# Query and key heads of the sparse attention: transposed two at a time in float32, split into parts from PSUM

## The chip, the cores and the metric

One core of a Trainium2 chip runs one decoder layer. The metric is the device time of one execution in microseconds (us).

## The reference, cut to what matters

The layer is h + half a SwiGLU, then a mixer of two head groups, then half a SwiGLU and a gated embedding; width 1024, 512 tokens, float32 throughout. The change is in the first head group, native sparse attention (NSA): 8 query heads of 64 in two groups of 4, and 2 key/value heads (one for each group) for each of two kinds, "selected" and "window".

```python
q_a = partial_rope(rmsnorm(split_heads(qa, N_HEADS_NSA), q_norm_nsa[i]), cos, sin)
k_slc = partial_rope(rmsnorm(split_heads(ksl, N_KV_NSA), k_norm_slc[i]), cos, sin)
k_win = partial_rope(rmsnorm(split_heads(kwn, N_KV_NSA), k_norm_win[i]), cos, sin)
...
s_c = jnp.einsum('bkgqd,bknd->bkgqn', qq, k_cmp) * scale
...
s_s = jnp.einsum('bkgqd,bkqnd->bkgqn', qq, kg) * scale
...
s_w = jnp.einsum('bkgqd,bknd->bkgqn', qq, kw) * scale
```

With 512 tokens, all 8 blocks are selected and the window covers all, so both kinds are full causal attention with different keys and values. The second head group (FoX, 8 heads) and the two SwiGLU blocks are not touched.

## The kernel before

Every product is made from float32 numbers split into two parts of type float32r: hi, a rounded copy (made by ScalarE), and lo, the rest (a subtraction on VectorE). A general product takes three matmuls (hi hi, hi lo, lo hi). A head has only 64 dimensions, so in attention its hi part and its lo part lie above each other in the 128 partitions: a query operand A holds hi and lo, and there are two key operands, B with hi and lo and B with the halves exchanged. Two matmuls over 128 partitions then give all four products.

The code does not write instructions in order. Each call goes to a planner (class Plan): `record` keeps the operation, its cost by formula and what it depends on; two instructions of different engines that touch the same PSUM tile are always put in order, whatever they do. `weave` mixes several streams of work, those with less TensorE cost so far first. `issue` then fixes the order on each engine by a greedy schedule with these costs, within a window of 440 operations, and `emit` (line 306) issues the instructions. So nearly every instruction in the profile stands at L306, and groups are told apart by engine, operation and tiles. Engines run their queues in order.

Names of tiles: `acc` and `gub` are the two sorts of PSUM bank, four of each; `k` is a 4 KB tile, here the operands A and B (also others); `hl` holds the two parts of heads before they are transposed, two buffers; `w` is a working tile of 2 KB; `st`, `hi` and `lo` are loaded weights and their parts; `s`, `r`, `cs` are small tiles; `x` is an 8 KB tile.

The mixer goes in this order: a projection for compression; then keys and values (`kv_project`), followed by the queries of group 0 (`q_project(0)`), woven with the compression's own products; then the compressed attention of group 0 and its first head pair, woven with the queries of group 1; then further pairs, woven with FoX projections and FoX pairs. For each of four tiles of 128 tokens a projection ends in `kv_done` or `q_done`: ScalarE scales the sums out of PSUM, squares them, VectorE sums the squares, POOL takes the inverse root (tile `s`, with `mhalf`), VectorE scales by it and by the gain, and POOL rotates the first 16 dimensions (`rope`, tiles `r` and `w`). What stands after the rotation is what changes:

- `split_heads` makes hi (ScalarE) and lo (VectorE) of four heads, side by side for each head, in `hl`;
- TensorE transposes each head's 128 columns (hi and lo together) into PSUM, four transposes into two `gub` banks;
- for queries (`qT`), ScalarE copies each bank into A in one go; for keys, three copies of a bank (one whole, two exchanged halves) go to B, for one kind on ScalarE and for the other on VectorE.

`A[g][a]` holds the heads 2a and 2a+1 of group g, and `B[kind][i]` both key heads of a kind. `cmp_attention` and `nsa_pair` read these.

Of the kernel before, what the change touches and what calls it, by code (L numbers as in the profile page):

```python
# [7 lines left out]
F32 = mybir.dt.float32  # L8
# [6 lines left out]
P = 128  # L15
# [293 lines left out]
class Layer:  # L309
# [471 lines left out]
    def parts(hl, hd, i):  # L781
        return hl[:, hd, i:i + 2].rearrange("p a d -> p (a d)").bitcast(F32)

    def qT(self, hl, heads, dst, t):

        nc = self.nc
        ps = self.gub()
        for i, hd in enumerate(heads):
            nc.tensor.transpose(ps[:, i * P:(i + 1) * P], self.parts(hl, hd, 0), self.ident)
        nc.scalar.copy(dst[:, :, t * P:(t + 1) * P], ps[:, :2 * P].rearrange("p (a c) -> p a c", a=2))  # L790

    def vsplit(self, src, dst, t):

# [182 lines left out]
    def cmp_attention(self, A, t, g, o):  # L976

        nc = self.nc
        ps = self.gub()
        pv = ps[:, :256].rearrange("p (h a n) -> p h a n", h=4, a=2)  # L980
        for hd in range(4):
            a = A[hd // 2][:, hd % 2, t * P:(t + 1) * P]
            nc.tensor.matmul(pv[:, hd], lhsT=a, rhs=self.kcT[:, :, g * 32:g * 32 + 32], start=True, stop=True)
        s = self.misc((P, 4, 32), "cs", 2)
        nc.vector.tensor_tensor(s, pv[:, :, 0], self.cmask[:, t, None, :].to_broadcast([P, 4, 32]), ALU.add)
        nc.vector.tensor_tensor(s, s, pv[:, :, 1], ALU.add)
        m, rs = self.small(4), self.small(4)
        nc.vector.tensor_reduce(m, s, axis=AX.X, op=ALU.max)
        bc = lambda x: x[:, :, None].to_broadcast([P, 4, 32])
        nc.gpsimd.tensor_tensor(s, s, bc(m), ALU.subtract)  # L990
        nc.scalar.activation(s, s, AF.Exp)
        nc.vector.tensor_reduce(rs, s, axis=AX.X, op=ALU.add)
        nc.vector.reciprocal(rs, rs)
        nc.vector.scalar_tensor_tensor(rs, rs, self.cval[:, t:t + 1], self.gates[:, t, 4 * g:4 * g + 4, 0],
                                       op0=ALU.mult, op1=ALU.mult)
        nc.gpsimd.tensor_tensor(s, s, bc(rs), ALU.mult)
        pt = self.gub()
        nc.tensor.transpose(pt[:, :P], s.rearrange("p h n -> p (h n)"), self.ident)
        pr = self.misc((P, 2, P), "cp", 2, F32R)
        nc.scalar.copy(pr[:, 0], pt[:, :P])  # L1000
        nc.vector.tensor_sub(pr[:, 1], pt[:, :P], pr[:, 0].bitcast(F32))
        po = self.gub()
        for i, (x, y) in enumerate(((0, 0), (0, 1), (1, 0))):
            nc.tensor.matmul(po[:, :256], lhsT=pr[:, x], rhs=self.vbd[:, g, y], start=(i == 0), stop=(i == 2))
        nc.scalar.copy(o[:, t, 256 * g:256 * g + 256], po[:, :256])
        yield
# [61 lines left out]
    def mix(self, xT, rs_in, o_nsa, o_fox, nsa_out):  # L1068
        nc = self.nc
        G, V = nc.gpsimd, nc.vector  # L1070
# [21 lines left out]
        B, Vt = {}, {}  # L1092

        def kv_project():
            for kind in range(2):
                Vt[kind] = self.k4((P, 2, NT, P), F32R)
                B[kind] = [self.k4((P, 2, 512), F32R) for _ in range(2)]

            def kv_done(t, ps):
                u = self.w2()  # L1100
                nc.scalar.mul(u, ps, rs_in[t])
                uv = u.rearrange("p (a s h d) -> p a s h d", a=2, s=2, h=2)
                for kind in range(2):
                    self.vsplit(uv[:, kind, 1], Vt[kind], t)
                xn = self.w2()[:, :256]
                x4 = xn.rearrange("p (a h d) -> p a h d", a=2, h=2)
                sq, ss = self.w2()[:, :256], self.small(4)
                nc.scalar.activation(sq.rearrange("p (a h d) -> p a h d", a=2, h=2), uv[:, :, 0], AF.Square)
                V.tensor_reduce(ss, sq.rearrange("p (n d) -> p n d", n=4), axis=AX.X, op=ALU.add)
                r = self.rstd(ss, 64, 4).rearrange("p (a h) -> p a h", a=2)  # L1110
                V.tensor_tensor(x4, uv[:, :, 0], r[:, :, :, None].to_broadcast([P, 2, 2, 64]), ALU.mult)
                V.tensor_tensor(x4, x4, self.gkv[:, :, None, :].to_broadcast([P, 2, 2, 64]), ALU.mult)
                xn = xn.rearrange("p (n d) -> p n d", n=4)
                self.rope(G, xn, t, 4)
                hl = self.split_heads(xn, 4, 2)
                cols = slice(t * P, (t + 1) * P)
                for kind in range(2):
                    tp = self.gub()
                    for i in range(2):
                        nc.tensor.transpose(tp[:, i * P:(i + 1) * P], self.parts(hl, 2 * kind + i, 0), self.ident)  # L1120
                    k = tp[:, :256].rearrange("p (a c) -> p a c", a=2)
                    copy = nc.scalar.copy if (t + kind) % 2 else V.tensor_copy
                    copy(B[kind][0][:, :, cols], k)
                    copy(B[kind][1][0:64, :, cols], k[64:128])
                    copy(B[kind][1][64:128, :, cols], k[0:64])
            yield from self.project(xT, [(768, 512)], kv_done, "v")

        A = {}

        def q_project(g):  # L1130
            A[g] = [self.k4((P, 2, 512), F32R) for _ in range(2)]

            def q_done(t, ps):
                u = self.w2()[:, :256].rearrange("p (h d) -> p h d", h=4)
                nc.scalar.mul(u, ps[:, :256].rearrange("p (h d) -> p h d", h=4), rs_in[t])
                xn = self.w2()[:, :256].rearrange("p (h d) -> p h d", h=4)
                self.head_norm(V, u, xn, self.gq[:, None, :].to_broadcast([P, 4, 64]))
                self.rope(G, xn, t, 4)
                hl = self.split_heads(xn, 4, 2)
                for i in range(2):  # L1140
                    self.qT(hl, (2 * i, 2 * i + 1), A[g][i], t)
            yield from self.project(xT, [(256 * g, 256)], q_done, f"q{g}")

        def cmp_group(g):
# [3 lines left out]
        def nsa_pair(g, a):  # L1148
            for kind in range(2):
                rs = self.rs_tile()  # L1150
                hd = 4 * g + 2 * a
                cols = slice(64 * hd, 64 * hd + 128)

                def write(ps, coef):
                    tmp = self.w2()
                    tv = tmp.rearrange("p (t h d) -> p t h d", t=NT, h=2)
                    V.tensor_mul(tv, ps, coef)
                    G.tensor_tensor(o_nsa[:, :, cols], o_nsa[:, :, cols],
                                    tmp.rearrange("p (t c) -> p t c", t=NT), ALU.add)
                run = lambda par: self.unit([(A[g][a][:, par], B[kind][i][:, g]) for i in range(2)], Vt[kind][:, g],  # L1160
                                            rs, par)
                yield from self.pair([run, run],
                                     rs, self.gates[:, :, hd:hd + 2, 1 + kind], write)
# [30 lines left out]
        def f_pair(p):  # L1194
# [7 lines left out]
            def write(ps, coef):  # L1202
# [9 lines left out]
                    self.forget_rows())  # L1212
        nc.weave(chain(kv, q_project(0)), cmp)
        streams = dict(c0=cmp_group(0), c1=cmp_group(1), n00=nsa_pair(0, 0), n01=nsa_pair(0, 1), n10=nsa_pair(1, 0),
                       n11=nsa_pair(1, 1), q1=q_project(1), out=nsa_out)
        for p in range(4):
            streams[f"F{p}"], streams[f"f{p}"] = f_project(p), f_pair(p)
# [335 lines left out]
```

## Time and profile before

| | us |
|---|---|
| median of 3 runs | 1086.06 (1085.07 to 1086.37) |
| profiled execution | 1086.81 |
| its span, first to last instruction | 1085.0 |

| engine | busy us | share of the span | instructions |
|---|---|---|---|
| PE (TensorE matmul) | 1068.3 | 98% | 6723 |
| PEld (its weight loads) | 963.0 | 89% | 6723 |
| DVE (VectorE) | 767.7 | 71% | 1320 |
| ACT (ScalarE) | 579.4 | 53% | 1115 |
| POOL (GpSimd) | 183.6 | 17% | 314 |

Times in rows count from the start of the span. The granted TensorE clock was 0.999 of full speed. Matmuls overlap each other (the next starts before the last one ends), so a busy time near the length of a stretch can hide small gaps. The mixer lies between about 310 and 690 us; the tiles of keys and queries that the change touches between 389 and 470 us.

### The profile page before, as it was taken

Reading aid. Unit: us, or ns where it says so; the run is one execution under the profiler, and the core shown is the slowest. Engines: PE = TensorE matmul, PEld = TensorE weight load, DVE = VectorE, ACT = ScalarE, POOL = GpSimd, SP = SyncE. Lnnn points to the kernel's source line nnn. Section 1 sums busy time; section 2 is a strip of 40 time slices with the busy share of each in tenths; the row PEclk is TensorE's granted clock in tenths of the full one; section 3 lists DMA queues with packets and bytes.
Section 4 is the critical chain, followed back from the end, with each engine's and each line's share of the span. In section 5 each row is a group of like instructions: output and inputs, shape, how many; then the busy total and the mean of one; then the engine's idle time right before and its main releaser. Section 6 shows DMA issues by size and latency. Waiting matters only on the chain.

```text
span 1085.0 us, 17692 instructions
## 1 busy us (share of the span) xinstructions
PE 1068.3 (98%) x6723; PEld 963.0 (89%) x6723; DVE 767.7 (71%) x1320; ACT 579.4 (53%) x1115; POOL 183.6 (17%) x314
## 2 busy tenths in 40 slices
PE   9999999999999999999999999999999999999998
PEld 6789899988997878999999888889989998899887
DVE  5976378744774777989889786977537784487473
ACT  5544145522543768988888864645315552255351
POOL 1010000000000246554344610310000000000000
PEclk9999999999999999999999999999999999999999
DMA  8496356643444622302102241686535674333421
GB/s 269 138 236 195 97 138 186 186 131 99 116 118 123 216 68 75 85 6 60 41 21 75 74 161 51 221 224 167 174 97 144 187 183 132 102 108 122 152 107 67
DMA packets 76420, 139.79 MB, mean 129 GB/s; under 512 B 13616, under 2 KB 33600, under 8 KB 76080
## 3 DMA queue, kind: packets, MB, share of 16 engines
q1 hardware_dynamic: 71376, 120.76, 34.3%
q0 software_dynamic: 4960, 17.91, 9.4%
q8 instruction: 53, 0.87, 0.3%
q14 instruction: 31, 0.25, 0.1%
HBM read 132.23 MB, written 6.42 MB: 128 GB/s over the span
## 4 chain that ended last, share of the span: by engine, by line
PE 82%; DVE 6%; ACT 3%; DMA 3%; POOL 3%; issue 3%; SPq 0%; ACTq 0%; POOLq 0%; DVEq 0%
PE acc L306 52%; PE gub L306 30%; DVE k L306 2%; DVE lo L306 2%; POOL s L306 1%; ACT k L306 1%; DVE w L306 1%; ACT w L306 1%; DMA pt<-in_quarters 1%; DMA k<-in_x 1%; POOL r L306 1%; DMA gq<-in_q_norm_nsa 1%; POOL w L306 1%; ACT hi L306 1%; DVE pt L306 0%
## 5 line engine op out<-in xcount | busy, mean ns | idle before, releaser
L306 PE MATMUL acc<-hi,k 128*128 128x512 f32 (+1 forms) x832 | 262.8, 389 | 1.7 <-ACT k L306 1.2
L306 ACT CAST hi<-st 128x1024 fp32r<-128x1024 f32 (+4 forms) x150 | 148.6, 991 | 179.6 <-PE acc L306 93.3
L306 DVE TENSOR_TENSOR lo<-st,hi 128x1024 fp32r<-128x1024 f32 (+4 forms) x150 | 171.6, 1146 | 64.7 <-ACT hi L306 64.4
L306 PE MATMUL acc<-hi,x 128*128 128x384 f32 (+3 forms) x720 | 199.4, 349 | 0.3 <-ACT hi L306 0.3
L306 PEld LDWEIGHTS acc<-hi,k 128*128 128x128 f32 x832 | 155.9, 188 | 33.0 <-ACT k L306 2.0
L306 PE MATMUL acc<-lo,k 128*128 128x512 f32 (+1 forms) x432 | 163.9, 383 | 0.5 <-DVE lo L306 0.5
L306 ACT CAST hi<-pt 128x1024 fp32r<-128x1024 f32 x68 | 71.3, 1049 | 159.9 <-PE acc L306 90.3
L306 PE MATMUL gub<-x,hi 128*128 128x256 f32 x816 | 147.4, 282 | 0.1
L306 PE MATMUL acc<-x,hi 128*128 128x256 f32 x816 | 147.2, 282 | 0.0
L306 DVE TENSOR_TENSOR lo<-pt,hi 128x1024 fp32r<-128x1024 f32 x68 | 83.1, 1222 | 80.3 <-ACT hi L306 80.3
L306 PE MATMUL gub<-k,hi 128*128 128x512 f32 (+1 forms) x560 | 138.2, 338 | 1.1 <-ACT hi L306 1.1
L306 PEld LDWEIGHTS acc<-hi,x 128*128 128x128 f32 x720 | 127.1, 189 | 11.1 <-ACT hi L306 0.4
L306 PEld LDWEIGHTS gub<-x,hi 128*128 128x128 f32 x816 | 126.1, 189 | 0.8 <-DVE w L306 0.3
L306 PE MATMUL acc<-lo,x 128*128 128x384 f32 (+3 forms) x360 | 125.1, 348 | 1.7 <-DVE lo L306 1.7
L306 PEld LDWEIGHTS acc<-x,hi 128*128 128x128 f32 x816 | 125.6, 188 | 0.0
L306 PE MATMUL gub<-x,lo 128*128 128x256 f32 x408 | 115.3, 283 | 0.0
L306 PE MATMUL acc<-x,lo 128*128 128x256 f32 x408 | 115.3, 283 | 0.0
L306 POOL DMA_DIRECT2D pt<-in_quarters x34 | 29.8, 877 | 477.4 <-DMA pt<-in_quarters 240.4
L306 PEld LDWEIGHTS gub<-k,hi 128*128 128x128 f32 x560 | 96.3, 189 | 12.6 <-ACT hi L306 1.6
L306 PE MATMUL gub<-k,lo 128*128 128x512 f32 (+1 forms) x280 | 94.5, 338 | 0.4 <-DVE lo L306 0.4
L306 PEld LDWEIGHTS acc<-lo,k 128*128 128x128 f32 (+1 forms) x432 | 79.4, 184 | 15.6 <-DVE lo L306 0.8
L306 PEld LDWEIGHTS gub<-x,lo 128*128 128x128 f32 x408 | 76.9, 188 | 0.0
(163 smaller groups left out, 1714.6 us busy)
## 6 DMA issues: line engine op xcount, KB each, us to landing
st<-in_quarters SPq DMA_DIRECT2D x51, 512.0 KB, 3.5
st<-in_ffn_wd SPq DMA_DIRECT2D x44, 512.0 KB, 4.9
pt<-in_quarters SPq DMA_DIRECT2D x34, 512.0 KB, 4.5
pt<-in_quarters POOLq DMA_DIRECT2D x34, 512.0 KB, 6.5
st<-in_quarters SPq DMA_DIRECT2D x32, 256.0 KB, 4.9
st<-in_w_in SPq DMA_DIRECT2D x48, 128.0 KB, 2.4
st<-in_first SPq DMA_DIRECT2D x16, 256.0 KB, 3.8
st<-in_w_in SPq DMA_DIRECT2D x8, 512.0 KB
```

Source lines behind the costliest of these rows:

```text
L306: getattr(getattr(self.nc, op.eng), m)(*a, **k)
```

## The change

The heads are no longer split before the transpose. `turned` transposes two heads of float32 numbers at once: the 64 columns of two neighbouring heads make 128 columns, so four heads take two transposes into one `gub` bank, and of each pair the even head comes out on partitions 0 to 63 and the odd one on 64 to 127. The parts are made from PSUM: for each half, ScalarE copies hi to the same partitions and VectorE subtracts hi from the PSUM value and writes lo to the other 64. The operands are therefore sorted by the half a head came out on: `A[g][par]` holds the heads par and par + 2 of group g (odd heads with lo above hi), and `B[g][i]` the key head g of both kinds. For keys the second operand is made in the same way from PSUM: hi on the other side by ScalarE, lo by VectorE. The readers in `cmp_attention` and `nsa_pair` index accordingly. FoX keeps `split_heads`.

```diff
-    def qT(self, hl, heads, dst, t):
-
-        nc = self.nc
+    def turned(self, x):
+
         ps = self.gub()
-        for i, hd in enumerate(heads):
-            nc.tensor.transpose(ps[:, i * P:(i + 1) * P], self.parts(hl, hd, 0), self.ident)
-        nc.scalar.copy(dst[:, :, t * P:(t + 1) * P], ps[:, :2 * P].rearrange("p (a c) -> p a c", a=2))
+        for i in range(2):
+            self.nc.tensor.transpose(ps[:, i * P:(i + 1) * P], x[:, 2 * i:2 * i + 2].rearrange("p a d -> p (a d)"),
+                                     self.ident)
+        return ps[:, :2 * P].rearrange("p (a c) -> p a c", a=2)
+
+    def qT(self, x, dst, t):
+
+        pv = self.turned(x)
+        for par in range(2):
+            r, o = slice(64 * par, 64 * par + 64), slice(64 - 64 * par, 128 - 64 * par)
+            d = dst[par][:, :, t * P:(t + 1) * P]
+            self.nc.scalar.copy(d[r], pv[r])
+            self.nc.vector.tensor_sub(d[o], pv[r], d[r].bitcast(F32))
...
         for hd in range(4):
-            a = A[hd // 2][:, hd % 2, t * P:(t + 1) * P]
+            a = A[hd % 2][:, hd // 2, t * P:(t + 1) * P]
...
                 self.rope(G, xn, t, 4)
-                hl = self.split_heads(xn, 4, 2)
+                pv = self.turned(xn)
                 cols = slice(t * P, (t + 1) * P)
-                for kind in range(2):
-                    tp = self.gub()
-                    for i in range(2):
-                        nc.tensor.transpose(tp[:, i * P:(i + 1) * P], self.parts(hl, 2 * kind + i, 0), self.ident)
-                    k = tp[:, :256].rearrange("p (a c) -> p a c", a=2)
-                    copy = nc.scalar.copy if (t + kind) % 2 else V.tensor_copy
-                    copy(B[kind][0][:, :, cols], k)
-                    copy(B[kind][1][0:64, :, cols], k[64:128])
-                    copy(B[kind][1][64:128, :, cols], k[0:64])
+                for g in range(2):
+                    r, o = slice(64 * g, 64 * g + 64), slice(64 - 64 * g, 128 - 64 * g)
+                    k = pv[r]
+                    nc.scalar.copy(B[g][0][r, :, cols], k)
+                    V.tensor_sub(B[g][0][o, :, cols], k, B[g][0][r, :, cols].bitcast(F32))
+                    nc.scalar.copy(B[g][1][o, :, cols], k)
+                    V.tensor_sub(B[g][1][r, :, cols], k, B[g][0][r, :, cols].bitcast(F32))
...
                 self.rope(G, xn, t, 4)
-                hl = self.split_heads(xn, 4, 2)
-                for i in range(2):
-                    self.qT(hl, (2 * i, 2 * i + 1), A[g][i], t)
+                self.qT(xn, A[g], t)
...
-                run = lambda par: self.unit([(A[g][a][:, par], B[kind][i][:, g]) for i in range(2)], Vt[kind][:, g],
+                run = lambda par: self.unit([(A[g][par][:, a], B[g][i][:, kind]) for i in range(2)], Vt[kind][:, g],
                                             rs, par)
```

## Rows read from the trace of the kernel before

**Rows 1.** The page: busy time of engines; shares of the chain that ended last.
```profile
PE 1068.3 (98%) x6723; PEld 963.0 (89%) x6723; DVE 767.7 (71%) x1320; ACT 579.4 (53%) x1115; POOL 183.6 (17%) x314
...
PE 82%; DVE 6%; ACT 3%; DMA 3%; POOL 3%; issue 3%; SPq 0%; ACTq 0%; POOLq 0%; DVEq 0%
```
**Rows 2.** Busy time by stretch: length, then PE, PEld, DVE, ACT, POOL.
```profile
385.00:395.00 10.00, 8.89 (x41) 6.96 (x40) 5.51 (x16) 4.05 (x11) 5.10 (x12) 1.00 0.01 2
425.00:435.00 10.00, 9.34 (x76) 8.68 (x76) 7.97 (x26) 7.80 (x19) 9.23 (x20) 1.00 0.32 78
435.00:445.00 10.00, 9.14 (x72) 8.23 (x70) 9.47 (x44) 9.82 (x38) 5.43 (x15) 1.00 0.21 55
445.00:465.00 20.00, 20.00 (x147) 19.28 (x146) 18.74 (x53) 18.55 (x55) 10.18 (x19) 1.00 0.33 82
...
445.00:645.00 200.00, 197.85 (x1290) 181.75 (x1289) 178.49 (x506) 170.44 (x483) 86.74 (x139) 1.00 0.22 64
```
**Rows 3.** The chain in order of time, 385 to 475 us: start, length, what.
```profile
389.32 0.41 ACT hl L306
389.76 0.44 DVE hl L306
...
390.24 0.66 PE gub L306 x4
...
431.00 0.41 ACT hl L306
...
436.35 0.42 ACT hl L306
436.79 0.42 DVE hl L306
...
442.23 0.39 PE gub L306
```
**Rows 4.** Waits, 360 to 440 us: total, times, longest.
```profile
ACT hl L306 <- POOL w L306: 3.9, 4, 1.5
...
PE gub L306 <- DVE hl L306: 1.5, 2, 1.1
```
**Rows 5.** Timeline of PE, transposes of a query tile: start, length, what.
```profile
427.59 0.66 PE L306 MATMUL gub<-ident,hl 128*128 128x128 f32 x4 [0.38 <-DVE hl L306]
428.08 1.04 PE L306 MATMUL gub<-ident,w 128*32 128x128 f32 x8
428.88 0.36 PE L306 MATMUL acc<-hi,x 128*128 128x256 f32 x1
```
**Rows 6.** Timeline of ACT, a query tile's split and the instruction after it.
```profile
455.63 0.40 ACT L306 CAST hl<-w 128x256 fp32r<-128x256 f32 x1
455.94 0.40 ACT L306 ACTIVATE w<-w,s 128x128 f32<-128x128 f32 x1
```
**Rows 7.** Timeline, reads of PSUM banks: a key tile; later `norm_pairs`.
```profile
390.71 1.29 DVE L306 CAST k<-gub 128x256 fp32r<-128x256 f32 x3 [0.20 <-PE gub L306]
...
390.93 1.13 ACT L306 CAST k<-gub 128x256 fp32r<-128x256 f32 x3 [0.89 <-PE gub L306]
...
671.34 0.62 ACT L306 CAST k<-gub 128x256 fp32r<-128x256 f32 x2
...
671.73 0.75 DVE L306 TENSOR_TENSOR k<-gub,k 128x256 fp32r<-128x256 f32 x2 [1.48 <-ACT k L306]
...
672.80 0.65 ACT L306 CAST k<-gub 128x256 fp32r<-128x256 f32 x2
```
**Rows 8.** Groups by form, whole span: busy us, mean ns, idle before.
```profile
L306 DVE CAST k<-gub 64x256 fp32r<-64x256 f32 x40 | 16.7, 417 | 0.6 <-PE gub L306 0.2
L306 ACT CAST k<-gub 64x256 fp32r<-64x256 f32 x40 | 14.6, 366 | 0.4
L306 DVE TENSOR_TENSOR hl<-w,hl 128x256 fp32r<-128x256 f32 x28 | 12.0, 430 | 7.8 <-ACT hl L306 7.6
L306 DVE TENSOR_TENSOR k<-gub,k 128x256 fp32r<-128x256 f32 x24 | 9.3, 414 | 3.3 <-ACT k L306 3.3
```

## The prediction

> **What bounds the kernel now.** I read the page first, for the engines' shares [rows 1]: TensorE has work in flight for 98% of the span, and the chain that ended last runs 82% over it. Whatever takes TensorE time away where TensorE sets the pace is therefore worth its full price. But 98% is a mean, so the second view was the busy time by stretch around the change [rows 2]. Three stretches differ. From 385 to 395 us and from 425 to 445 us (keys, then the queries of group 0) TensorE is busy only 8.89, 9.34 and 9.14 of 10 us, and at 435 to 445 us ScalarE (9.82) and VectorE (9.47) are fuller than it is. From 445 to 465 us (queries of group 1 beside the first attention pair) TensorE is at 20.00 of 20. From 445 to 645 us, the rest of the mixer, it is at 197.85 of 200. Matmuls overlap, so even 9.1 of 10 hides small gaps. The third view, the chain in order of time for the early stretch, shows what the keys and queries wait for [rows 3]: at 389.32 us a split on ScalarE (0.41), at 389.76 the subtraction on VectorE (0.44), and only then the four transposes. At 431.00 and 436.35 us the split of a query tile is on the chain again, on ScalarE, and once more its subtraction at 436.79. So here the chain is one of small steps on several engines, and TensorE waits; TensorE's own waits name the same steps [rows 4].
>
> **What the change touches.** Twelve token tiles go through it: four of keys (kv_done), four for each of the two query groups (q_done). The first key tile's split starts at 389.32 us, the fourth query tile of group 0 at 436.35 us, and group 1 follows from 445 to 470 us. From 470 us on the work is the same instruction for instruction (operands indexed otherwise, same shapes); only the planner's order may differ.
>
> **TensorE.** Each tile loses two of its four 128x128 transposes: 24 in all. Price of one: eight transposes issued at 428.08 us are followed by the next matmul at 428.88, so 0.10 us each; the four at 427.59 take until 428.08, 0.12 each [rows 5]. The saving is 24 x 0.10 = 2.4 us (2.9 at the other price), 0.8 for the keys and 0.8 for each query group. In the stretch of group 1 TensorE is full, so I count its 0.8 whole. In the other two it is not full, and I count nothing for transposes there but price the chain.
>
> **ScalarE and VectorE, by instruction.** Costs are start to start, since neighbours overlap: the 256-column split on ScalarE holds it 0.31 us (455.63 to 455.94) [rows 6]; two 256-column subtractions on VectorE take 0.75 [rows 7], one alone 0.41 [rows 8], so the second starts 0.34 after the first. The new forms read 64 partitions of PSUM. Copies of that shape take 0.366 us on ScalarE and 0.417 on VectorE, and a subtraction from PSUM with 128 partitions takes 0.414 against 0.430 for the one from SBUF that goes [rows 8]. I therefore price the new 64x256 subtraction, which no row shows, like the old one. Its bounds are nothing gained and, at the far end, its whole length with nothing overlapping, 0.42, some 0.6 us more over eight.
> A query tile had one split and two copies on ScalarE and one subtraction on VectorE; now it has two copies and two subtractions. That is -0.31 on ScalarE and +0.34 on VectorE: -2.5 and +2.7 us over eight tiles.
> A key tile had a split and three copies on ScalarE, a subtraction and three copies on VectorE; now it has four copies on one and four subtractions on the other. Counts are equal, so the cost is about nothing. It hides behind nothing, it simply replaces like by like.
>
> **The wait in front of the transposes.** They now need POOL's rotation instead of split and subtraction. For the first key tile that takes 0.41 + 0.44 = 0.85 us off the chain [rows 3]. The subtraction comes after the transposes instead, where nobody waits: the key tiles are wanted by score matmuls of the attention pair, behind the query tiles. Between 0 (POOL's wait is merely handed on, ScalarE waited 3.9 us in four places for it [rows 4]) and 1.5 us (all that TensorE waited for these subtractions [rows 4]) I take 0.85. What is queued behind a transpose that waits on POOL is the projection's next matmuls; that is the danger in this edit.
> For queries of group 0 the chain from 431 to 437 us lies mostly on ScalarE, the fuller engine there. I take its four lost splits, 4 x 0.31 = 1.2 us. The bounds are -2.0 (transposes too) and +1.4 (VectorE's four more subtractions all on the path, 4 x 0.34).
>
> **PSUM.** Before, a bank of a key tile was read by one engine: the three copies on VectorE from 390.71 and the three on ScalarE from 390.93 ran at the same time, on two banks [rows 7]. After, one bank is read by both engines in eight steps. How this program treats that is seen where a bank is already split half by half: ScalarE's two copies at 671.34, VectorE's two subtractions at 671.73, and only at 672.80 ScalarE again [rows 7]. Eight steps in turn are 4 x (0.37 + 0.42) = 3.2 us instead of 1.3 on two engines. I take 0 as its price on the path, because the keys are wanted later and other work can fill the turns; the bound is the 1.9 us for the last key tile, if the two queues stand still.
> The Trainium skill, PSUM — Partial Sum Buffer, section Terms, says that two engines on the same bank and the same 32-partition quadrant at once are an error, reads against reads included, so taking turns is not a choice. The order in the pairs' rows agrees with it. By that rule alone the time would be that of the third rival below.
>
> **Sum.** -0.8 (group 1, TensorE) - 0.85 (first key tile) - 1.2 (group 0, ScalarE) = -2.85 us. The profiled execution took 1086.81 us, 1085.0 of it the span; it becomes 1083.96. It lies 0.75 us above the median of 1086.06, so the time shown should be 1083.2. Its own range goes from 1081.6 (all bounds on the good side: 1.0, 1.5 and 2.0) to 1085.3 (group 1's 0.8 alone); above that it is another case.
>
> **Rivals.**
> First, nothing that can be told: the gain on ScalarE and in front of the transposes is eaten by waits that were hidden behind it (POOL's power and rotation, which feed every tile and stay), and only the 0.8 of group 1 is left. That gives 1085.3. For it speaks that POOL's steps are late by themselves; against it that split and subtraction stand on the chain by name.
> Second, slower: VectorE becomes the pacer. Place: 427 to 470 us, where eight more subtractions of 0.34 land, 2.7 us. VectorE is idle 0.53 us of 10 at 435 to 445 and 1.26 of 20 at 445 to 465 [rows 2]. It decides once the subtractions that fall in those two stretches pass 1.8 us of room, or stand in front of a softmax step that TensorE waits for. With all of it on the path and none of the savings, 1086.06 + 2.7 = 1088.8. Against it: VectorE had 2 us to spare at 425 to 435 and the order is made anew with these costs known.
> Third, the turns on a bank hold up both queues for the last key tile: +1.9, less group 1's 0.8, so 1087.2.
> That the change does not do what it says is hardly possible: the instructions are counted from the code, with no branch.
>
> **How the numbers follow.** A measurement of this kernel can tell about 0.2%, 2.2 us, from no change. My case has 0.62; with its weight falling evenly from 1083.2 to both ends of its range, three quarters, 0.46, lie below 1083.9, and 0.16 counts as same. The first rival has 0.18, same. The second has 0.12, slower. The third has 0.08: 0.05 slower when a query tile is held up too, 0.03 same. So faster 0.46, same 0.37, slower 0.17. The range reaches past the case's own lower end by half of the 1.2 (a new order may also recover small gaps that the modelled busy time hides), 1081.0, and up beyond the third rival to 1087.6; about 0.08 is left out below and 0.10 above.
>
> **What would show it.** Right: 24 fewer transposes; ScalarE's eight splits of queries gone and VectorE with 1328 instructions instead of 1320; TensorE's waits for the split's subtraction gone between 385 and 445 us; the stretch up to the start of TensorE's solid part (442 us on the chain) shorter by about 2 us, and some 0.8 more by 470. Wrong: TensorE waiting on POOL's rotation there for over 1.5 us in sum; VectorE above 9.7 of 10 from 435 to 465 with the chain on it; ScalarE and VectorE waiting for each other in key tiles; or a gap from 470 to 645 us that was not there, which would be the new order and not the change.

## The result, and the profile after

The changed kernel takes 1092.41 us (median of 4 runs, 1089.77 to 1093.09); the kernel before, measured with it, took 1085.57 (1083.95 to 1086.37). The ratio is 1.0056 [1.004, 1.0072]: slower by 6.8 us, where 2.85 less had been forecast, and outside the range. The profiled execution took 1093.09 us with a span of 1091.3, at a mean granted clock of 0.991; that of before had a span of 1085.0 at 0.999.

The page first: busy time of the engines, the clock that TensorE was granted in 40 slices of the span, and the shares of the chain that ended last.

```profile
PE 1070.9 (98%) x6699; PEld 966.4 (89%) x6699; DVE 772.5 (71%) x1328; ACT 577.8 (53%) x1106; POOL 182.5 (17%) x314
...
PEclk9999999999999997999999999999999999999999
...
PE 87%; DVE 4%; ACT 3%; DMA 2%; POOL 2%; issue 1%; SPq 0%; ACTq 0%; POOLq 0%; DVEq 0%
```

TensorE has 24 instructions fewer than in [rows 1] and yet 2.6 us more of busy time, and one digit of the clock is a 7. That slice, the 16th, is 409 to 437 us, where the queries of group 0 are made. The busy time by stretch (PE, PEld, DVE, ACT, POOL, granted clock) says more, beside [rows 2]. The first line is a stretch of the kernel before that is not shown there, the others are of the changed kernel:

```profile
415.00:425.00 10.00, 9.36 (x77) 8.95 (x75) 7.92 (x18) 8.55 (x21) 6.14 (x10) 1.00 0.00 1
...
415.00:425.00 10.00, 6.37 (x50) 5.72 (x50) 8.59 (x18) 8.59 (x21) 6.55 (x7) 0.95 0.00 1
...
424.00:426.00 2.00, 0.00 (x0) 0.00 (x0) 1.31 (x3) 0.00 (x0) 1.83 (x4) 0.50 0.00 0
...
425.00:435.00 10.00, 8.63 (x40) 8.29 (x41) 5.81 (x17) 2.29 (x7) 6.33 (x14) 0.50 0.01 2
435.00:445.00 10.00, 10.00 (x64) 9.57 (x64) 4.84 (x18) 5.82 (x14) 1.59 (x5) 0.70 0.06 14
```

From 424 to 426 us TensorE runs nothing, and the clock is 0.50 of full speed (1.2 instead of 2.4 GHz) from 424 until about 441 us. At 425 to 435 us TensorE runs 40 matmuls in 8.63 us of busy time where before it ran 76 in 9.34: a busy share alone would have hidden this, the count and the clock show it. ScalarE and VectorE fall to 2.29 and 5.81 of 10; in a run below that keeps this order and the full clock they are at 5.81 and 9.62, so they are short of work from TensorE here and do not hold it up.

What TensorE waited for stands in its timeline (start, length, what, and in brackets the idle time before it with its releaser):

```profile
422.25 0.38 PE L306 MATMUL acc<-hi,x 128*128 128x256 f32 x1
426.37 0.69 PE L306 MATMUL gub<-ident,w 128*128 128x128 f32 x2 [3.74 <-POOL w L306]
426.70 0.56 PE L306 MATMUL acc<-lo,k 128*64 128x256 f32 x1
```

The two transposes are those of the second query tile of group 0. They now read the rotated tile `w` itself, TensorE's queue runs in order, and behind them stand matmuls of other work: the next, `acc<-lo,k`, needs a part that VectorE had finished at 423.51 us (422.30 and 1.21, below), and stood for some 2.9 us behind the transposes. Why the rotation was late is seen on POOL, first in a quiet stretch, then here, and on VectorE:

```profile
386.61 0.32 POOL L306 TENSOR_TENSOR r<-w,cos 128x64 f32<-128x64 f32 x1 [1.00 <-DVE w L306]
386.89 0.51 POOL L306 TENSOR_TENSOR r<-w,sin 128x32 f32<-128x32 f32 x2
...
422.12 1.70 POOL L306 TENSOR_TENSOR r<-w,cos 128x64 f32<-128x64 f32 x1 [0.73 <-DVE w L306]
423.79 1.85 POOL L306 TENSOR_TENSOR r<-w,sin 128x32 f32<-128x32 f32 x2
...
425.99 0.32 POOL L306 TENSOR_TENSOR w<-r,r 128x64 f32<-128x64 f32 x1
```

```profile
422.30 1.21 DVE L306 TENSOR_TENSOR lo<-x,hi 128x1024 fp32r<-128x1024 f32 x1
...
424.10 1.21 DVE L306 TENSOR_TENSOR lo<-st,hi 128x1024 fp32r<-128x1024 f32 x1
```

The same three instructions took 0.83 us for the first key tile and 3.55 us here, where two subtractions of 1024 columns, both operands in SBUF, ran on VectorE meanwhile. The Trainium skill, SBUF — State Buffer, section Who interferes with whom, states that a VectorE instruction with two SBUF inputs contends with a GpSimd instruction that reads SBUF, and that the other side blocks for the whole instruction. The lengths agree with it (1.70 us beside a subtraction of 1.21 where a quiet one takes 0.32), though POOL's row starts 0.18 us ahead of the subtraction's; no run here took those subtractions away, so that cause is argued, not shown.

The waits of 360 to 440 us, against [rows 4]:

```profile
PE gub L306 <- POOL w L306: 7.5, 4, 3.7
...
DVE k L306 <- ACT k L306: 13.2, 12, 3.6
```

Where TensorE waited 1.5 us for the heads' subtraction, it now waits 7.5 us for the rotation. In [rows 4] the rotation's lateness (3.9 us) was a wait of ScalarE's split, with nothing of TensorE behind it in the queue.

How far the work had come, by the scaling of the fourth query tile and the first softmax reduction of the attention pair. First of the kernel before, then of the changed one:

```profile
426.98 0.47 ACT L306 ACTIVATE w<-acc,s 128x256 f32<-128x256 f32 x1
...
432.04 0.28 DVE L306 CUSTOM_DVE_ANT_0 w<-gub,mask 128x128 f32<-128x128 f32 x1
```

```profile
423.24 0.47 ACT L306 ACTIVATE w<-acc,s 128x256 f32<-128x256 f32 x1
...
440.48 0.28 DVE L306 CUSTOM_DVE_ANT_0 w<-gub,mask 128x128 f32<-128x128 f32 x1
```

Just before the stall the changed kernel was 3.74 us ahead; at the first reduction it is 8.44 us behind. At the eighth reduction it is 12.0 us behind (464.14 against 452.14); by the 96th, the last, 6.3 (637.61 against 631.28), which is the difference of the spans. Not all of this is time lost, because the new order also does other work earlier. What is lost shows against a run described below that keeps the changed kernel's order without the long wait (one tile's rotation on VectorE):

```profile
433.75 0.28 DVE L308 CUSTOM_DVE_ANT_0 w<-gub,mask 128x128 f32<-128x128 f32 x1
```

Behind that run the changed kernel is 6.73 us at the first reduction, 8.16 at the eighth (455.98 there) and 8.17 at the 96th (629.44). The whole loss is there by the eighth reduction, and nothing later adds to it. The order by itself is 3.84 us behind the kernel before at the eighth reduction and 1.84 us ahead at the 96th: that is the 5.7 us that the changed kernel seems to get back.

### The profile page after: what moved, and what is told of

Read it like the earlier page. It is cut to its first block, busy times and chain, and to the rows that moved or that the text cites. A ratio compares the mean times of both kernels' runs of the same rounds, so it can differ in the third digit from the quotient of the medians.

```text
span 1091.3 us, 17667 instructions
## 1 busy us (share of the span) xinstructions
PE 1070.9 (98%) x6699; PEld 966.4 (89%) x6699; DVE 772.5 (71%) x1328; ACT 577.8 (53%) x1106; POOL 182.5 (17%) x314
## 4 chain that ended last, share of the span: by engine, by line
PE 87%; DVE 4%; ACT 3%; DMA 2%; POOL 2%; issue 1%; SPq 0%; ACTq 0%; POOLq 0%; DVEq 0%
PE acc L306 54%; PE gub L306 33%; DVE k L306 1%; DVE lo L306 1%; POOL r L306 1%; DVE w L306 1%; DMA st<-in_first 1%; ACT w L306 1%; POOL s L306 1%; DMA st<-in_quarters 1%; ACT k L306 1%; ACT hi L306 1%; DMA gq<-in_q_norm_nsa 1%; SPq L306 0%; POOL w L306 0%
## 5 line engine op out<-in xcount | busy, mean ns | idle before, releaser
L306 PE MATMUL acc<-hi,x 128*128 128x384 f32 (+3 forms) x720 | 204.8, 355 | 0.0
L306 PEld LDWEIGHTS acc<-hi,x 128*128 128x128 f32 x720 | 130.3, 194 | 11.2 <-ACT hi L306 0.2
```

The source lines that it names most:

```text
L306: getattr(getattr(self.nc, op.eng), m)(*a, **k)
```

## The experiments

The first theory was that of the timeline: the wait on POOL in TensorE's queue and the clock that fell behind it. Its rivals were the eight bank turns of the key tiles, and later the order that the planner makes anew whenever anything changes. All medians are to be compared with that of before on the same chip, 1085.04 to 1085.92.

**Keys alone and queries alone.** Each takes the changed half and leaves the other as before, `run` indexing accordingly (queries alone is shown):

```diff
-                pv = self.turned(xn)
+                hl = self.split_heads(xn, 4, 2)
...
-                run = lambda par: self.unit([(A[g][par][:, a], B[g][i][:, kind]) for i in range(2)], Vt[kind][:, g],
+                run = lambda par: self.unit([(A[g][par][:, a], B[kind][i][:, g]) for i in range(2)], Vt[kind][:, g],
```

> Only the queries are changed; keys are split before the transpose as in the kernel before. Stall theory: the long wait of the changed kernel (3.74 us, TensorE on POOL's rotation, then the clock at half until 441 us) stands at a query tile, so it can recur: if a wait of over 3 us is there the clock falls and the time is 1088 to 1092; if the new order happens to avoid it, 1083 to 1086 with the clock at 1.00. Rival, turns on a PSUM bank: the eight alternating steps are the keys' and are gone, so 1084 to 1086 whatever TensorE waits for.

Queries alone took 1092.19 us (ratio 1.0055 [1.004, 1.0071]), which neither theory had foreseen without a wait of over 3 us.

> Only the keys are changed; queries as in the kernel before. Stall theory: the key tiles' waits on POOL (1.99 us the longest) stay, too short for the clock, so about 1085 to 1088 with the clock at 1.00. Rival, turns on a PSUM bank: all of the loss is here, 1090 to 1093. Rival, VectorE too full: eight subtractions fewer than in the changed kernel, 1084 to 1086.

Keys alone took 1091.19 us (1.0046 [1.0031, 1.0061]), above the forecast of the stall theory, with waits of TensorE on the rotation of 3.4 us in 385 to 480 us. The clock fell twice, to 0.83 in 405 to 415 us, behind a wait of 1.99 us at a key tile (404.95 us), and to 0.83 in 425 to 435 us. So such a wait is not too short for the clock, as had been expected; in the changed kernel the same wait, 1.99 us at 404.59, left it at 1.00. Each half costs nearly the whole, so they do not add. The time of keys alone would fit the rival of the turns, but queries alone has no key turns: the turns are not needed for a loss. Queries alone also speaks against the wait on POOL as the only cause: its waits on the rotation in 385 to 480 us sum to 1.0 us, and its profiled clock was 0.998 with a span of 1088.6 (3.6 over before's). At its 64th reduction it is 1.13 us ahead of before; it falls behind after that, and its longest wait stands where the change touches nothing:

```profile
618.75 1.11 PE L306 MATMUL gub<-ident,x 128*128 128x128 f32 x4 [2.62 <-ACT k L306]
```

The clock is 0.85 at 615 to 620 us and 0.81 at 620 to 625 there, where before has 1.00. So another order can make the same sort of loss, a wait and then a slower clock, at another place. This was the fastest of its four executions; the others had clocks of 0.996 and 0.997 and were not profiled.

**Transposes put later.** The planner, which knows the rotation by its quiet price, counts the new transposes as ready 3 us later and so puts other matmuls ahead of them:

```diff
-                o.ready = max(o.ready, fin + op.lat[o.eng])
+                o.ready = max(o.ready, fin + op.lat[o.eng] + o.late)
...
+        self.nc.late = 3000.0
```

> The whole change; in the planner alone, the two transposes of each of the 12 tiles count as ready 3.0 us later than POOL's rotation by its formula, so they are issued behind other matmuls. Nothing else differs. Stall theory: TensorE's waits on POOL's rotation fall from 7.7 us to under 2, the clock stays at 1.00, and the time is 1082 to 1086. Rivals (turns on a bank; VectorE too full): those instructions are all still there, so 1089 to 1093.

It took 1098.77 us (1.0109 [1.0091, 1.0127]), far outside what was expected. The waits on the rotation are gone, but the clock still fell (0.83 at 415 to 425 us), and TensorE is busy only 34.67 of 40 us from 445 to 485, in waits of at most 0.9 us on several producers. Why this order is so much worse was not followed up. Distance is no free cure.

**Rotation on VectorE.** For all 12 tiles, `self.rope(V, xn, t, 4)` in place of `G`; the order is planned anew.

> The whole change; the rotation of keys and queries runs on VectorE instead of POOL, so the transposes wait for VectorE and the rotation is no longer slowed beside VectorE's large subtractions (1.70 and 1.85 us against 0.32 and 0.47). VectorE gets 48 small instructions more, some 8 us. Stall theory: no wait of over 2 us, clock at 1.00, 1083 to 1087. Rival, VectorE too full: 1093 or more, with VectorE on the chain.

It took 1088.07 us (1.0018 [1.0009, 1.0027], 10 runs), 4.3 less than the changed kernel but above the 1083 to 1087 expected, though the clock was 1.000 in eight of the ten executions and TensorE's waits for VectorE's rotation were 1.5 us in sum. The order is another too, so this run alone decides nothing.

**Two edits that keep the changed kernel's order.** The instructions are issued in exactly its order. The first keeps the wait and fills it: 16 bf16 matmuls on zeros, read by nobody, ahead of the second query tile's transposes. The second takes the wait's cause away: that one tile's four rotation instructions go to VectorE at their places in the order.

```diff
+            if op.mark is not None:
+                for _ in range(16):
+                    self.nc.tensor.matmul(op.mark[:], lhsT=self.dummy[:, :P], rhs=self.dummy[:], start=True, stop=True)
```

```diff
-            getattr(getattr(self.nc, op.eng), m)(*a, **k)
+            getattr(getattr(self.nc, op.mark or op.eng), m)(*a, **k)
...
+                nc.mark = "vector" if g == 0 and t == 1 else None
```

> The changed kernel in its own order; 16 matmuls on zeros (128x512, bf16) are added in front of the two transposes of the second query tile of group 0, into the bank that the transposes then write, so that TensorE works while POOL rotates. It does work that nothing uses. The wait stays, what is taken away is the idle TensorE. Theory that the clock is the larger part of the loss: the granted clock stays at 1.00 from 424 to 441 us, and the time is 1085 to 1089. Rival, the wait itself is the loss: 1091 to 1093. Rival, the new order is the loss whatever the clock: 1090 to 1093, with the clock at 1.00.

> The changed kernel in its own order on TensorE, ScalarE and the queues; the four rotation instructions of the second query tile of group 0 alone are issued on VectorE at their place instead of on POOL. Stall theory: TensorE's wait of 3.74 us shrinks to under 1.5, the clock stays at 1.00, the time is 1083 to 1088. Rival, the new order is the loss: 1090 to 1093 with the clock at 1.00.

The filled kernel's stall in TensorE's timeline, and its stretches:

```profile
423.50 3.40 PE L310 MATMUL gub<-dummy 128*128 128x512 bf16 x15
427.15 0.44 PE L312 MATMUL gub<-ident,w 128*128 128x128 f32 x2 [0.26 <-POOL w L312]
```

```profile
425.00:435.00 10.00, 9.74 (x73) 8.13 (x72) 7.09 (x20) 3.39 (x10) 7.65 (x15) 1.00 0.01 2
435.00:445.00 10.00, 10.00 (x84) 9.56 (x83) 8.64 (x38) 9.40 (x30) 3.19 (x7) 1.00 0.53 129
```

The transposes come no earlier (427.15 against 426.37), but in the profiled execution the clock stays at 1.00, and at 435 to 445 us 84 matmuls run where 64 did (of the 73 at 425 to 435, some 8 are still the filling: 1.9 us of it at 3.40 / 15 = 0.23 each). The time is 1088.72 us (1.002 [1.0011, 1.0029], 10 runs), the profiled span 1085.9. The wait is still there, so what the filling gives back is the clock: 3.7 us in the medians (1092.41 - 1088.72; 4.0 when each is taken against the kernel before on its own chip) and 5.4 us in the profiled spans (1091.3 - 1085.9).

With the rotation on VectorE the same wait is shorter:

```profile
424.54 0.44 PE L308 MATMUL gub<-ident,w 128*128 128x128 f32 x2 [1.53 <-DVE w L308]
```

```profile
425.00:435.00 10.00, 10.00 (x84) 9.33 (x84) 9.62 (x30) 5.81 (x16) 6.03 (x13) 1.00 0.01 2
```

The time is 1087.6 us (ratio 1.0016 [0.9996, 1.0036], 10 runs); the profiled span is 1083.3 at a clock of 1.000, 8.0 less than the changed kernel's and 1.7 less than before's. But its runs reach from 1084.74 to 1093.14 us, and they follow the clock: the four fastest, 1084.74 to 1087.15, had 1.000, 1.000, 0.998 and 0.998, the four slowest, 1089.17 to 1093.14, had 0.997, 0.995, 0.992 and 0.994. Of one and the same program some executions lost the clock and some did not. So this edit does not always keep the clock; where it was kept, the whole loss is gone.

**More rotations moved, same order.** All 12 tiles, and then the two with the longest waits (`t == 2` of the keys beside the one above).

> The changed kernel in its own order on TensorE, ScalarE and the queues; the rotation of all 12 tiles (48 instructions) is issued on VectorE at its place. Stall theory: no wait of TensorE on POOL is left, none over 1.5 us on VectorE, clock 1.00 in nearly all executions, 1082 to 1087. Rival, VectorE becomes too full with some 8 us more: above 1089 with the clock at 1.00.

> As the one with one tile's rotation on VectorE, and the rotation of the third key tile as well: the two longest waits on POOL (3.74 and 1.99 us) are taken away, the order kept. Stall theory: clock 0.998 or more in nearly all executions, 1083 to 1086, and no execution above 1090. Rival, the clock falls for another reason than these waits: executions at 0.995 and less stay, at 1089 to 1093.

All 12: 1088.07 us (1.0031 [1.0019, 1.0043]), 1 us above what was expected; the longest wait at these transposes is 1.5 us, and still the clock is 0.61 at 425 to 435 us. Two: 1087.3 us (1.0015 [1.0004, 1.0025]); the clock did not stay above 0.998 as expected, the profiled execution had 0.66 there. Neither has a long wait left. What both have is a thin stretch ahead of it; the windows of two tiles moved:

```profile
415.00:425.00 10.00, 7.14 (x57) 6.29 (x57) 8.63 (x22) 8.85 (x21) 5.97 (x7) 1.00 0.00 1
425.00:435.00 10.00, 10.00 (x58) 9.71 (x59) 6.82 (x20) 3.02 (x9) 4.88 (x10) 0.66 0.01 2
```

In the kernel before, TensorE is busy 9.36 of 10 us at 415 to 425. The changed order came there earlier, perhaps ahead of the engines that feed TensorE; no run tested that.

**The order by itself.** To see what a new order costs with no change of the work, the planner's price of a matmul is moved by 0.1 ns or more, in the kernel before and in the changed one:

```diff
-            return f * max(m / 1.2, self.cols(outs[0]) / 2.4) + 2.5
+            return f * max(m / 1.2, self.cols(outs[0]) / 2.4) + 2.6
```

> The kernel before, the planner's formula for a matmul raised by 0.1 ns (2.5 to 2.6): the same instructions, in a slightly different order in the mixer. Theory that this order is a lucky one and any new order costs: 1087 to 1092. Rival, order by itself costs little: 1085 to 1086.5.

> The changed kernel with the same 0.1 ns. Theory that the loss is one stall that the order happened to make: a run without a wait of over 3 us and without a fall of the clock, 1083 to 1088. Theory that transposes which wait for POOL stall in any order: a wait of over 2 us again, 1088 to 1093.

> The kernel before, the planner's formula for a matmul lowered by 0.1 ns (2.4): a second other order of the same instructions. Theory that the order decides and that of the kernel before is a good one: 1087 to 1092. Rival, the other order with 2.6 was an exception: 1085 to 1086.5.

> The changed kernel with the same 2.4. Theory that the order decides, and that the change by itself is worth little: 1086 to 1093, within 3 us of the kernel before at 2.4. Rival, the change by itself costs some 6 us: 1093 or more when that one is at 1087 or more.

> The kernel before, the planner's formula for a matmul at 2.7 ns: a further order of the same instructions. Theory that the order of the kernel before is a good one among its neighbours: 1086.5 to 1091. Rival, three orders of four are like the first: 1085 to 1086.

> The changed kernel at 2.7 ns. Theory that the change adds nothing by itself and only draws another order: as often below as above the kernel before at 2.7, say within 5 us of it. Theory that transposes waiting straight on POOL make orders worse: above it by 3 to 10 us, with a wait on POOL of over 3 us or a clock below 0.997.

The last pair tells the planner that a small POOL instruction of the rotation's sort takes twice as long, nearer to what it takes beside VectorE:

```diff
-            return 300 + 165 * n if a[-1] == ALU.pow else 130 + 2.1 * n
+            return 300 + 165 * n if a[-1] == ALU.pow else (130 + 2.1 * n) * (2 if n <= 64 else 1)
```

> The kernel before; the planner counts POOL's rotation at twice its formula (528, 394, 528 ns; the trace has 528, 281, 466 in this stretch, the formula 264, 197, 264). Theory that the planner's too small price for POOL makes TensorE wait: 1084 to 1086. Rival, order alone: 1086 to 1091.

> The changed kernel with POOL's rotation at twice the formula. Theory that TensorE stalls because the planner believes POOL to be early: TensorE's waits on POOL below 3 us in sum and none over 2, clock 0.998 or more, 1083 to 1087. Rival, order alone: anything from 1086 to 1097, whatever the sum of these waits.

Medians in us, and what TensorE waited for these transposes at 385 to 480 us in the profiled execution:

| planner's number | before | changed | changed - before | wait before, sum | wait changed, sum (longest) |
|---|---|---|---|---|---|
| 2.5 (as given) | 1085.57 | 1092.41 | +6.8 | 1.5 | 7.7 (3.7) |
| 2.6 | 1090.51 | 1087.9 | -2.6 | 1.8 | 4.3 (2.0) |
| 2.4 | 1087.0 | 1097.53 | +10.5 | 1.5 | 7.9 (3.7) |
| 2.7 | 1086.59 | 1086.67 | +0.1 | 1.5 | 4.8 (2.0) |
| POOL doubled | 1087.84 | 1092.37 | +4.5 | 0.9 | 1.1 (1.1) |

Two things follow. An order alone moves the kernel before by 4.9 us (4.6 against the kernel before on the same chip), and its own order is the best of its five. And the five differences have a mean of +3.9 us with a standard deviation of 5.2, so a standard error of 2.3: the sign points to a cost of the change in an average order, but five pairs do not show it. The longer waits on the rotation are seen in four pairs of five: 4.3 to 7.9 us against 1.5 to 1.8. The two orders with a wait of 3.7 us are slow, the two whose longest is 2.0 us are within 3 us of before's own time. A wait is not yet a loss: at 2.7 the 4.8 us of waits left the profiled clock at 1.000 and the time like that of the kernel before at 2.7, while at 2.6 the clock fell behind a wait of 1.99 us (0.64 at 406 to 409 us). At 2.4 the changed kernel is 10.5 us slower, not within 3 as the first theory had it; its profiled execution (1092.22 us) was the fastest of four, and what the others, 1097.04 to 1100.08 us at clocks of 0.990 to 0.993, met was not seen. With POOL doubled both expectations of the theory failed: the kernel before gained nothing (1087.84), and in the changed one the wait is gone as foreseen, and the time is 1092.37 all the same. Its stretches:

```profile
420.00:425.00 5.00, 3.88 (x22) 3.20 (x22) 3.89 (x12) 4.33 (x10) 3.32 (x5) 0.83 0.01 2
425.00:430.00 5.00, 5.00 (x24) 5.00 (x24) 4.38 (x12) 1.44 (x5) 4.11 (x6) 0.50 0.00 0
```

TensorE is thin again (3.88 of 5), in small waits of at most 0.8 us on the projection's own operands, and the clock falls to 0.50 for 5 us.

## Why the prediction was wrong, point by point

- **TensorE**: right in its count. The transposes of `hl` went from 112 to 64 and those of `w` from 288 to 312, so 24 fewer.
- **ScalarE and VectorE, by instruction**: right. VectorE has 1328 instructions, and the new subtraction from 64 partitions of PSUM takes 0.422 us where the price was 0.41 to 0.42:

```profile
L306 DVE TENSOR_TENSOR k<-gub,k 64x256 fp32r<-64x256 f32 x32 | 13.5, 422 | 12.1 <-ACT k L306 11.4
```

- **The wait in front of the transposes**: this step failed. It took a gain of 0.85 us and bounded it at 0 to 1.5 us of gain, with no end on the side of a loss. The same paragraph named what stands behind a transpose that waits on POOL, the next matmuls of other work, and called it the danger, but gave it no price. It measured 7.5 us of waiting instead of 1.5, with one wait of 3.74 us, and half a clock from 424 to 441 us. The reasoning counted what leaves the chain (split and subtraction) and not that these two instructions had kept POOL's lateness out of TensorE's queue. Filling that wait gives back 3.7 us and shortening it 4.8 us, out of a difference of 6.8 us. For the order that was timed, these two experiments show the wait and the clock behind it as the larger part of the loss. The 1.7 to 2.8 us that the two edits leave above the kernel before lie at least in part in executions whose clock fell all the same.
- **Group 0's splits (-1.2) and group 1's transposes (-0.8)**: something of the sort was there. Up to 423 us the changed kernel was 3.74 us ahead, more than the 0.85 + 1.2 = 2.05 forecast for keys and group 0 together. This is not clean, since the order differs too: what is done earlier there is in part paid back later. TensorE is also thinner after the lead, 6.37 of the 7.63 us from 415 us to the stall. The repair that keeps the order had a clock of 1.000 in two of ten executions, and they end at 1084.74 and 1085.07 us, about 1 us under before's 1085.92 and not 2.85.
- **PSUM**: taken at 0 and not contradicted. VectorE did wait 13.2 us for ScalarE in the key and query turns, but all these turns are still there in the executions at 1084.74 and 1085.07 us. One reading does not hold: that ScalarE comes back to the bank only at 672.80 [rows 7] need not be a turn, because it was busy with another split from 671.86 on (`hi<-st`, 1.06 us).
- **The rivals**: none was it. VectorE as the pacer would have shown VectorE fuller at 425 to 445 us; it was emptier (5.81 and 4.84 of 10 us), and in the filled kernel, at the full clock, it is at 7.09 and 8.64 while TensorE is at 9.74 and 10.00. The first rival had POOL's lateness eat up the gain, not turn it into a loss. The sign that the prediction gave for being wrong, TensorE waiting on POOL's rotation for over 1.5 us in sum, is what came; it had been written down without a rival that carried it.

Open: why the clock falls in some executions of a program and not in others, why queries alone and the doubled price are slow in their orders, and whether the change costs time in an average order. No order tried with the change beat the kernel before in its own order; the nearest are 1086.67 us (price 2.7, ratio 1.0009 [1.0, 1.0019]) and 1087.3 us (two rotations moved).

## What to carry to other kernels

When a change removes the step between a late producer and TensorE, the lateness moves into TensorE's in-order queue: price the wait by the producer's slow case, with everything queued behind it, and add what half a clock can cost afterwards (3.7 us here). An engine that gains a lead can lose more than the lead, if the lead ends in a pause. A lag at one place of two different orders is not yet a loss: compare runs of the same order. Where a planner rewrites the whole order, time several orders of both kernels before a difference of 0.5% is put down to the edit: here an order alone was worth 4.9 us.

## What the runs showed of the hardware

- POOL's three rotation products took 0.83 us in a quiet stretch and 3.55 us beside two long subtractions on VectorE.
- In the changed kernel TensorE idled from 422.63 to 426.37 us, after 6.37 us of work in the 7.63 before. The granted clock fell during that idle time and not after it: it was 1.00 up to 423.5 us and 0.50 (1.2 GHz) from 424 to about 441 us, though TensorE was busy again from 426.4 us. With the idle time filled, the profiled execution shows 1.00 throughout. The Trainium skill, TensorE: Matmul & The Clock Gate, section What's actually happening, describes a gate with these two levels, and the rows agree (1.00 and 0.50).
- Behind a wait of 1.99 us at a key tile the clock stayed at 1.00 in the changed kernel and fell with keys alone (0.53 at 406 to 409 us). It also fell without one long wait. With two rotations moved, TensorE had run 7.14 of 10 us before a stretch at 0.66; with one moved, 7.23 of 10 before a stretch at 1.00, and another execution of that same program had a mean clock of 0.992.
